# Two pairs of value projections as 1024-wide groups, in a one-core decoder layer

## The chip, the core and the metric

The kernel runs on one core of a Trainium2 chip. A core has a matrix engine (TensorE, called PE in the profile; its weight loads are PEld), a vector engine (DVE), a scalar engine with lookup tables (ACT), a general engine (POOL) and a queue engine (SP). Each works through its own instructions in order and waits for the others by semaphores. PE reads operands from on-chip memory (SBUF) and writes sums to banks of PSUM. The metric is the device time of one execution in microseconds.

## The reference

One layer: a normed input `h` (512 tokens, 1024 features) times one wide matrix `w_in`, whose columns are split for two token mixers; their outputs are gated, merged and projected; then an MLP and a gated extra projection. What matters here:

```python
h = rmsnorm(x, ln1[i])
hq, hk, hv, hr, ha, hatt, hgate = _split_cols(h @ w_in[i], SPLIT_SIZES)
log_a = jax.nn.log_sigmoid((ha @ w_a2[i] + b_a[i]).astype(jnp.float32)) / GLA_TAU
o = gla_mixer(hq..., hk..., hv..., log_a...)     # gated linear attention: 4 heads, values 4 x 256
...
o = o * gla_gn[i] * jax.nn.silu(hr)              # the gate r
...
hatt = hatt.reshape(B, S, N_ATT_GROUPS, 3, ATT_HEADS_PER_GROUP, ATT_HEAD_DIM)   # q, k, v of 3 groups
for g, (win, dil) in enumerate(ATT_GROUPS):      # dilations 1, 4, 16
    o_g, lse_g = dilated_attention(hatt[:, :, g, 0], hatt[:, :, g, 1], hatt[:, :, g, 2], ...)
wts = jax.nn.softmax(jnp.stack(lses, axis=0), axis=0)
o_att = jnp.sum(wts[..., None] * jnp.stack(outs, axis=0), axis=0).reshape(B, S, ATT_W)
```

The columns that the change touches are the values of attention groups 1 and 2 (512 columns each) and the values of the linear attention (1024 columns). The linear attention works in chunks of 64 tokens: per head a running sum of the gate (the "decay"), its exponentials, and queries and keys multiplied by them.

## The kernel before

**Precision.** A float32 product is made of three reduced-precision ones. Each operand is split into `hi` (a rounded copy) and `lo` (what is left), and PE adds hi·hi, lo·hi and hi·lo.

**Weights.** They come as operands of 128 x 1024 (512 KB each). For each, SP issues the load, ACT makes `hi` (L244) and DVE makes `lo` (L239). There are 6 buffers for raw weights, 5 for hi and 4 for lo.

**Groups.** 512 x 1024 x 512 projections are done in seven block products in place of eight (`strassen`, L301). Each of the seven stages has one weight operand: the blocks A11, A12, A22 themselves or sums of blocks (S1 = A21 + A22, S2 = S1 + A11, S3 = A11 + A21, S4 = S2 + A12), against blocks of `h` and their sums (T1 to T4). The order is A11, S1, A22, S2, A12, S4, S3. S1 is a load by SP to which POOL adds a second load in memory (an accumulating DMA, L210); S3 likewise, onto A11 (L221); S2 and S4 are sums on DVE in place (L218, L224). A stage is 24 matmuls of 128 moving columns by 256 (4 inner blocks, 2 halves, 3 products). After stages 0 to 3 ACT copies a bank out (`begin`, L332), after stages 4 to 6 DVE adds the rest (`end`, `add`, L350). Two layouts exist: features on partitions (`quad`), and tokens on partitions (`quadt`, for values), where the weight is the moving operand.

**Order of work.** The program is one stream per engine, laid out by the code itself. `run` (L255) issues matmuls in pieces of eight, and after each piece `step` pops one closure from a list `later` (copies, additions, splits) and, whenever enough columns have been issued (`pace`), takes one step of one of two side generators: scores and softmax, attention values, decay, linear attention. `fetch` issues, whenever an operand is wanted, the lo split of the second operand ahead, the hi split of the third, the sums of the fourth and the loads of the fifth. An engine thus sees splits, evacuations and side work in one fixed order, and a side instruction that waits or takes long holds the splits behind it.

**Around the change.** The groups run in the order k1, q2, k2, v1, v2, v0, gq, gk, gv0, the attention's output projection (`oa`), r0, gv1, r1, then the merge gates. During v1 the scores of groups 1 and 2 are made (`scores12`); at its end their softmax sums go to DRAM and back in another shape (`s_dram`, L713 and L715, both on POOL) and PE transposes them (L719). v1 and v2 are written to DRAM (L658) and read back sorted by residue class (L664). Attention values (`pv`), merge coefficients (`weights`) and `decay` (L851, L852) run beside v0 to gv0, the first linear-attention heads (`gla`, L865) beside `oa` and r0, the last two beside r1. Of a head's steps, the first four prepare: exponentials on ACT (L870, L881, L882), products and copies on DVE (L871 to L895). The gate r is x·sigmoid(x): `silu` issues a sigmoid on ACT (L1051) and two products on DVE (L1055). ACT must load a table whenever it changes between exponential and sigmoid.

## Time and profile before

| what | us |
|---|---|
| median of 3 runs | 965.95 (965.8 to 965.99) |
| the profiled execution | 966.74 |
| its span, first to last instruction | 964.9 |
| PE busy in the span | 956.2 (99%) |
| DVE busy | 745.4 (77%) |
| ACT busy | 537.4 (56%) |
| POOL busy | 104.0 (11%) |
| v1: 144.10 to 171.32 | 27.22 |
| gv0: 270.31 to 293.59 | 23.28 |
| r0: 320.88 to 346.57 | 25.69 |
| gv1: 346.57 to 368.28 | 21.71 |
| r1: 368.28 to 388.53 | 20.25 |

A matmul's line shows its modelled duration; matmuls overlap, so the pace is read from their starts. "Idle before" is what an engine lost ahead of a line's instructions, with what ended most of it. The granted TensorE clock is 0.998 of full speed over the whole execution.

### The profile page before, as it was taken

The numbers are of one execution on the slowest core, as the hardware profiler recorded it, in microseconds if no ns is written. First come the engines' busy times: TensorE is split into PE (matmuls) and PEld (weight loads), VectorE is DVE, ScalarE is ACT, GpSimd is POOL, SyncE is SP. The second block draws the span as 40 slices with busy tenths as digits, with TensorE's granted clock in tenths as the row PEclk, the third lists the DMA queues.
The fourth block names the chain that finished last, engine by engine and source line by source line (L and its number), as shares of the span: only waits on it lengthen the run. The fifth ranks groups of instructions, "written<-read, shape, count | busy, mean of one in ns | idle before, by whom it ended". The sixth has DMA issues, their size and how long they took to land.

```text
span 964.9 us, 16746 instructions
## 1 busy us (share of the span) xinstructions
PE 956.2 (99%) x6732; PEld 893.7 (93%) x6732; DVE 745.4 (77%) x1068; ACT 537.4 (56%) x878; POOL 104.0 (11%) x145
## 2 busy tenths in 40 slices
PE   9999999999999999999999999999999999999997
PEld 7789999999998999999988899999998998988886
DVE  7787879676788769978955788777767899787754
ACT  7346546445666677665732446555655674345633
POOL 0140010420001021013001000010000100000000
PEclk9999999999999999999999999999999999999999
DMA  8565555874446646455536437556654474563102
GB/s 294 159 201 128 153 135 129 236 199 135 110 109 186 164 102 157 113 154 182 169 91 205 119 78 185 153 140 168 170 158 109 113 180 103 132 196 108 44 1 88
DMA packets 41470, 138.93 MB, mean 144 GB/s; under 512 B 5363, under 2 KB 6975, under 8 KB 41392
## 3 DMA queue, kind: packets, MB, share of 16 engines
q1 hardware_dynamic: 27936, 93.29, 29.6%
q0 software_dynamic: 12160, 42.20, 22.1%
q10 hardware_dynamic: 1296, 2.36, 0.7%
q8 instruction: 53, 0.87, 0.4%
q14 instruction: 25, 0.20, 0.1%
HBM read 131.50 MB, written 8.17 MB: 145 GB/s over the span
## 4 chain that ended last, share of the span: by engine, by line
PE 97%; DVE 1%; issue 1%; DMA 1%; ACT 0%; SPq 0%; POOLq 0%; POOL 0%; DVEq 0%; ACTq 0%
PE mmt L258 84%; PE smt L258 4%; PE smt L863 1%; PE smt L803 1%; PE smt L728 1%; DMA u<-in_xT_dram 1%; PE mmt L478 1%; PE mmt L479 0%; PE mmt L477 0%; PE smt L701 0%; PE smt L820 0%; PE smt L819 0%; PE smt L809 0%; PE smt L700 0%; PE smt L991 0%
## 5 line engine op out<-in xcount | busy, mean ns | idle before, releaser
L258 PE MATMUL mmt<-ur,hi 128*128 128x256 f32 (+1 forms) x3152 | 645.3, 302 | 0.0
L258 PEld LDWEIGHTS mmt<-ur,hi 128*128 128x128 f32 x3152 | 506.0, 188 | 24.8 <-issue 1.9
L258 PE MATMUL mmt<-ur,lo 128*128 128x256 f32 (+1 forms) x1576 | 476.9, 303 | 0.0
L239 DVE TENSOR_TENSOR lo<-w,hi 128x1024 fp32r<-128x1024 f32 x251 | 304.2, 1218 | 49.5 <-PE mmt L258 32.1
L244 ACT ACTIVATE hi<-w 128x1024 fp32r<-128x1024 f32 x251 | 262.5, 1054 | 93.2 <-PE mmt L258 28.0
L258 PEld LDWEIGHTS mmt<-ur,lo 128*128 128x128 f32 x1576 | 296.8, 188 | 11.9 <-issue 0.4
L258 PE MATMUL mmt<-hi,ur 128*128 128x256 f32 (+3 forms) x736 | 153.7, 305 | 0.0
L357 ACT ACTIVATE ur<-u 128x512 fp32r<-128x512 f32 x132 | 78.5, 624 | 105.3 <-DVE u L1098 30.9
L258 PEld LDWEIGHTS mmt<-hi,ur 128*128 128x128 f32 x736 | 118.5, 189 | 5.6
L350 DVE TENSOR_TENSOR u<-u,mmt 128x512 f32<-128x512 f32 (+1 forms) x124 | 78.3, 657 | 44.8 <-PE mmt L258 44.6
L258 PE MATMUL mmt<-lo,ur 128*128 128x256 f32 (+3 forms) x368 | 112.2, 305 | 0.0
L365 DVE TENSOR_TENSOR ur<-u,ur 128x512 fp32r<-128x512 f32 x131 | 86.2, 684 | 17.6 <-ACT ur L357 16.9
L332 ACT ACTIVATE u<-mmt 128x512 f32<-128x512 f32 x104 | 61.6, 592 | 55.8 <-PE mmt L258 55.5
L258 PEld LDWEIGHTS mmt<-lo,ur 128*128 128x128 f32 x368 | 69.4, 188 | 2.7
L221 POOL DMA_DIRECT2D w<-in_wts_dram x28 | 24.9, 890 | 356.2 <-DVE w L218 258.3
L210 POOL DMA_DIRECT2D w<-in_wts_dram x28 | 25.8, 921 | 276.5 <-DVE ur L365 52.8
L258 PE MATMUL smt<-ur,hi 128*128 128x512 f32 x144 | 44.7, 390 | 0.1
L224 DVE TENSOR_TENSOR w<-w 128x1024 f32<-128x1024 f32 x28 | 34.3, 1225 | 1.0
L218 DVE TENSOR_TENSOR w<-w 128x1024 f32<-128x1024 f32 x28 | 34.3, 1225 | 1.0
L258 PEld LDWEIGHTS smt<-ur,hi 128*128 128x128 f32 x144 | 26.9, 188 | 6.0 <-DVE ur L365 0.5
L258 PE MATMUL smt<-ur,lo 128*128 128x512 f32 x72 | 28.2, 391 | 0.0
L390 ACT ACTIVATE u<-u 128x512 f32<-128x512 f32 x24 | 14.9, 622 | 16.5 <-DVE u L1179 16.5
(210 smaller groups left out, 715.0 us busy)
## 6 DMA issues: line engine op xcount, KB each, us to landing
w<-in_wts_dram SPq DMA_DIRECT2D x167, 512.0 KB, 4.2
w<-in_wts_dram POOLq DMA_DIRECT2D x56, 512.0 KB, 5.8
u<-in_xT_dram SPq DMA_DIRECT2D x8, 256.0 KB, 5.1
v_dram<-u POOLq DMA_DIRECT2D x8, 256.0 KB, 6.2
u<-v_dram POOLq DMA_DIRECT2D x8, 256.0 KB, 6.6
y_dram<-u ACTq DMA_DIRECT2D x8, 256.0 KB, 2.4
u<-y_dram POOLq DMA_DIRECT2D x8, 256.0 KB, 6.0
u<-in_xT_dram POOLq DMA_DIRECT2D x8, 256.0 KB, 8.6
```

The lines of the kernel that those rows point to most:

```text
L210: GP.dma_start(w, wts[UNIT[f"{q}.A22"]], accum_op=OP.add)
L218: V.tensor_tensor(w, w, raw[f"{q}.A11"], op=OP.add)
L221: GP.dma_start(w, wts[UNIT[f"{q}.A21"]], accum_op=OP.add)
L224: V.tensor_tensor(w, w, raw[f"{q}.A12"], op=OP.add)
L239: V.tensor_tensor(lo, w, hi.bitcast(F32), op=OP.subtract)
L244: S.activation(hi, w, AF.Copy)
L258: TE.matmul(o, lhsT=l, rhs=r, start=a, stop=b, skip_group_check=shared)
L332: S.activation(sums[c], bank[b], AF.Copy, scale=-scale if c[0] else scale)
L350: V.tensor_tensor(out, s, ps, op=OP.subtract if m else OP.add)
L357: S.activation(hi, x, AF.Copy)
L365: V.tensor_tensor(lo, x, hi.bitcast(F32), op=OP.subtract)
L390: S.activation(t, x, AF.Square, scale=1.0 / 32.0)
```

## The change

v1 and v2 become one group `v12`, gv0 and gv1 one group `gv`, each of 1024 features with tokens on partitions. A new function `wide` does the seven products with weight operands of twice the width: two units each (`.0`, `.1`), moving rows of 512 columns, two PSUM banks for each accumulator, and a `step` after every three matmuls. The order of its products is A11, S1, S2, A12, S3, S4, A22. S3 is no longer summed onto the loaded A11, but comes by a load of its own on SP (A11 again) with POOL's accumulation of A21 on it; the table `EARLY` says how many operands ahead the accumulating loads are issued.

The moved work: `gla(0)` and `gla(1)` are put beside gv (before: beside `oa`), `gla(2)` and `gla(3)` beside `oa` and r0 (before: beside r1). They wait in the program for the decay and the values they need. The values of the attention groups are kept in two DRAM buffers. `scores12` has one more `yield` per head. The third sum operand T3 is split into buffers that q1 leaves.

```diff
+    def quadw(name, src, cs):
+        for m, k in ((0, 0), (1, 0), (1, 1), (0, 1)):
+            for i in range(2):
+                u.append((f"{name}.A{m + 1}{k + 1}.{i}", "quadw", src, 2 * i + k, cs[m]))
...
-    quad("v1", "w_in", att_col(1, 2), "quadt")
-    quad("v2", "w_in", att_col(2, 2), "quadt")
+    quadw("v12", "w_in", (att_col(1, 2), att_col(2, 2)))
...
-    quad("gv0", "w_in", GV, "quadt")
+    quadw("gv", "w_in", (GV, GV + 512))
...
-    quad("gv1", "w_in", GV + 512, "quadt")
...
+WIDE = (("A11", "B11", "a"), ("S1", "T1", "c"), ("S2", "T2", "a"), ("A12", "B21", "b"), ("S3", "T3", "a"),
+        ("S4", "B22", "c"), ("A22", "T4", "a"))
+WBEGIN = {0: ((0, 0), "a"), 1: ((1, 1), "c"), 2: ((0, 1), "a")}
+WEND = {3: ((0, 0), "b"), 4: ((1, 1), "a"), 5: ((0, 1), "c"), 6: ((1, 0), "a")}
...
-EARLY = {max(i - LEAD, 0): n[:-4] for n, i in OPERAND.items() if n.endswith(".A11")}
+def early():
+    after_wide = False
+    for n, i in OPERAND.items():
+        q, _, what = n.partition(".")
+        if what == "S1":
+            EARLY.setdefault(max(i - (4 if after_wide else 7), 0), []).append((n, f"{q}.A21", f"{q}.A22"))
+            after_wide = False
+        elif what[:3] == "S1.":
+            EARLY.setdefault(i - 4, []).append((n, f"{q}.A21.{what[3:]}", f"{q}.A22.{what[3:]}"))
+            after_wide = True
+        elif what[:3] == "S3.":
+            EARLY.setdefault(i - 2, []).append((n, f"{q}.A11.{what[3:]}", f"{q}.A21.{what[3:]}"))
...
-            step(PIECE * r.shape[-1])
+            step(n * r.shape[-1])
...
+    def wide(name, xo, finish):
...
+        for i, (op, xname, b) in enumerate(WIDE):
+            fresh = b not in bank
+            if fresh:
+                bank[b] = [smt() if b == "b" else mmt() for _ in range(2)]
+            for pr in range(4):
+                wh, wl = weight(f"{name}.{op}.{pr // 2}")
+                xh, xl = xo(xname, pr)
+                r = slice((pr % 2) * 512, (pr % 2 + 1) * 512)
+                mms = []
+                for n in range(2):
+                    c = slice(n * P, (n + 1) * P)
+                    for k, (l, w) in enumerate(((xh, wh), (xl, wh), (xh, wl))):
+                        mms.append((bank[b][n], l[:, c], w[:, r], fresh and not pr and not k, pr == 3 and k == 2))
+                run(mms, 3, shared=True)
+            if i in WBEGIN:
+                (m, t), b = WBEGIN[i]
+                later[0:0] = [begin(m, t, n, b) for n in range(2)]
+            if i in WEND:
+                (m, t), b = WEND[i]
+                later.extend(end(m, t, n, b) for n in range(2))
...
     def gla(h):
+        while len(gb_) <= h:
+            yield
...
+        while len(gv) < 8:
+            yield
+        if h == 2:
+            for p in range(4):
+                split_later(gv[1, p], gv, (1, p))
...
-    gv = [values("gv0", True)]
-    drain()
+    gv = {}
+    side.extend(gla(h) for h in range(2))
+    values_parts("gv", gv)
+    flush()
     pace[0] = 4096
-    side.extend(gla(h) for h in range(2))
+    side.extend(gla(h) for h in range(2, 4))
...
-    gv.append(values("gv1", True))
-    flush()
-    side.extend(gla(h) for h in range(2, 4))
```

How the order of instructions changes at three places (line numbers of the changed kernel: L239 the accumulating load, before L210; L272 the lo split, before L239; L277 the hi split, before L244).

On POOL, where the softmax sums leave for DRAM (`s_dram`), before:

```order
L210 DMA w_1500<-in_wts_dram 128x1024
L221 DMA w_1437<-in_wts_dram 128x1024
L210 DMA w_1807<-in_wts_dram 128x1024
L713 DMA s_dram_1841<-st12_323 128x8x4
L715 DMA u_1843<-s_dram_1841 32x128
L658 DMA v_dram_1600<-u_1672 128x2x256
L221 DMA w_1714<-in_wts_dram 128x1024
```

and with the change, where w_1805 is the first sum S1 of the group v0, and the two loads ahead of it are the S3 of v12:

```order
L239 DMA w_1640<-in_wts_dram 128x1024
L239 DMA w_1678<-in_wts_dram 128x1024
L239 DMA w_1805<-in_wts_dram 128x1024
L814 DMA s_dram_1824<-st12_326 128x8x4
L816 DMA u_1826<-s_dram_1824 32x128
L759 DMA v0_dram_1596<-u_1686 128x512
```

Before, the load ahead of `s_dram` was one of v2's; now it is one of v0's, into a buffer of v12.

On DVE in gv, with the change: the lo splits of A12.1 (lo_3111), S3.0, S3.1 and S4.0 (lo_3195), the two sums for S4 (L248), and between them the preparation of head 1 (L974 to L998, before L871 to L895):

```order
L272 TENSOR_TENSOR lo_3111<-w_3023,hi_3079 128x1024
L974 TENSOR_TENSOR u_3128<-u_2660 128x4x64
L976 TENSOR_TENSOR u_3129<-u_2660 128x4x64
L272 TENSOR_TENSOR lo_3135<-w_2990,hi_3113 128x1024
L248 TENSOR_TENSOR w_2618<-w_2618,w_2993 128x1024
L981 COPY dec_3150<-u_3127 128x8
L982 TENSOR_TENSOR u_2242<-u_2242,u_3127 128x512
L272 TENSOR_TENSOR lo_3164<-w_3020,hi_3137 128x1024
L248 TENSOR_TENSOR w_2669<-w_2669,w_3023 128x1024
L991 TENSOR_TENSOR u_3175<-u_2611,u_3128 128x512
L992 TENSOR_TENSOR u_2611<-u_2611,u_3129 128x512
```

Before, these rows of heads 0 and 1 stood behind the last lo split of gv0, among oa's.

On ACT at the end of r0, before: one table load ahead of r0's sigmoids (L1051):

```order
L244 ACTIVATE hi_3886<-w_3462 128x1024
L1051 ACT_TABLE_LOAD
L1051 ACTIVATE u_3921<-u_3724 128x512
L964 ACTIVATE u_3862,gsq_3860<-smt_3866 128x256 x2
L244 ACTIVATE hi_3950<-w_3839 128x1024
L1051 ACTIVATE u_3973<-u_3850 128x512
```

and with the change (L1163 is the sigmoid, L973 the first exponential of heads 2 and 3, L984 the next one):

```order
L1163 ACT_TABLE_LOAD
L1163 ACTIVATE u_3863<-u_3686 128x512
L973 ACT_TABLE_LOAD
L973 ACTIVATE u_3875<-u_2736 128x512
L277 ACTIVATE hi_3883<-w_3809 128x1024
L1163 ACT_TABLE_LOAD
L1163 ACTIVATE u_3906<-u_3820 128x512
L973 ACT_TABLE_LOAD
L973 ACTIVATE u_3908<-u_2797 128x512
L1163 ACT_TABLE_LOAD
L1163 ACTIVATE u_3926<-u_3739 128x512
L1163 ACTIVATE u_3928<-u_3777 128x512
```

The exponentials of the two heads now stand between the sigmoids, each behind a table load of its own.

More of the change, by code (lines that the diff above doesn't have):

```diff
@@ L126, in operand_order @@
             names += [f"{name[:-3]}{a}" for a, _, _ in STAGES]
+        elif name.endswith("A11.0"):
+            names += [f"{name[:-5]}{a}.{i}" for a, _, _ in WIDE for i in range(2)]
     return names
@@ L189, in step, with flush @@
                 side.insert(min(WAYS - 1, len(side)), g)
+    def flush():
+        while later:
+            later.pop(0)()
     def drain():
@@ L206, in prepare @@
         name = OPERANDS[i]
-        if i in EARLY:
-            q = EARLY[i]
-            w = raw[f"{q}.S1"] = load(f"{q}.A21")
-            GP.dma_start(w, wts[UNIT[f"{q}.A22"]], accum_op=OP.add)
+        for n, a, b in EARLY.get(i, ()):
+            w = raw[n] = load(a)
+            GP.dma_start(w, wts[UNIT[b]], accum_op=OP.add)
         if name in UNIT:
@@ L214, in sums @@
     def sums(i):
-        q, _, what = OPERANDS[i].rpartition(".")
-        if what == "S2":
+        q, _, what = OPERANDS[i].partition(".")
+        if what[:3] in ("S2.", "S4."):
+            a, b = ("S1", "A11") if what[1] == "2" else ("S2", "A12")
+            w = raw[OPERANDS[i]] = raw[f"{q}.{a}{what[2:]}"]
+            V.tensor_tensor(w, w, raw[f"{q}.{b}{what[2:]}"], op=OP.add)
+        elif what == "S2":
             w = raw[f"{q}.S2"] = raw[f"{q}.S1"]
@@ L534, in xsums @@
         yield from sums(lambda g, p, o: V.tensor_tensor(t3[g][:, o], x(g, p, 1, 1), x(g, p, 0, 1), op=OP.subtract))
-        yield from splits("T3", t3)
+        while not q1_done:
+            yield
+        for g in range(2):
+            for p in range(2):
+                S.activation(xs[4 * g + 2 * p][0][:, halves(1)], t3[g][:, halves(p)], AF.Copy)
+        yield
+        for g in range(2):
+            for p in range(2):
+                hi, lo = cols(xs[4 * g + 2 * p], halves(1))
+                V.tensor_tensor(lo, t3[g][:, halves(p)], hi.bitcast(F32), op=OP.subtract)
+        yield
+    q1_done = []
     def xs_op(name, pr):
+        if name == "T3":
+            return cols(xs[2 * pr], halves(1))
         if name in ("B11", "B21", "B22"):
@@ L898, in gla @@
         yield
-        vh = [cols(gv[h // 2][h % 2, p // 2], halves(p % 2)) for p in range(4)]
+        while len(gv) < 8:
+            yield
+        if h == 2:
+            for p in range(4):
+                split_later(gv[1, p], gv, (1, p))
+        while not all(isinstance(gv[h // 2, p], tuple) for p in range(4)):
+            yield
+        vh = [cols(gv[h // 2, p], halves(h % 2)) for p in range(4)]
         kc = slice(0, 3 * P)
```

64 lines of the change are left out of this document (43 added, 21 removed).

## The prediction

> **What bounds the kernel now.** I read the page's totals first, then its chain of waits, then the costliest groups with what ended their idle time.
>
> ```profile
> span 964.9 us, 16746 instructions
> ...
> PE 956.2 (99%) x6732; PEld 893.7 (93%) x6732; DVE 745.4 (77%) x1068; ACT 537.4 (56%) x878; POOL 104.0 (11%) x145
> ...
> PE 97%; DVE 1%; issue 1%; DMA 1%; ACT 0%; SPq 0%; POOLq 0%; POOL 0%; DVEq 0%; ACTq 0%
> ...
> L258 PE MATMUL mmt<-ur,hi 128*128 128x256 f32 (+1 forms) x3152 | 645.3, 302 | 0.0
> ...
> L239 DVE TENSOR_TENSOR lo<-w,hi 128x1024 fp32r<-128x1024 f32 x251 | 304.2, 1218 | 49.5 <-PE mmt L258 32.1
> L244 ACT ACTIVATE hi<-w 128x1024 fp32r<-128x1024 f32 x251 | 262.5, 1054 | 93.2 <-PE mmt L258 28.0
> ```
>
> PE is busy 99% of the span, the chain is PE for 97% of it, and its main matmul line never waited (0.0 us). So every stall of PE that the change creates is added to the end, and the only gain there can be is PE time. VectorE and ScalarE make the operands, and part of their idle time is spent waiting for PE, so they run ahead. DVE has far less room than the 77% suggests in the stretches that the change rebuilds:
>
> ```profile
> core 0: us, PE busy (x) PEld busy (x) DVE busy (x) ACT busy (x) POOL busy (x), PEclk, DMA share, GB/s
> 144.10:171.32 27.22, 27.22 (x235) 27.22 (x233) 25.27 (x32) 17.01 (x43) 3.73 (x6) 1.00 0.52 119
> 270.31:293.59 23.28, 23.28 (x201) 23.28 (x199) 19.75 (x24) 12.28 (x18) 0.00 (x0) 1.00 0.59 152
> 320.88:346.57 25.69, 25.69 (x218) 25.69 (x217) 16.88 (x26) 14.97 (x29) 1.72 (x2) 1.00 0.53 131
> 368.28:388.53 20.25, 20.25 (x173) 20.25 (x172) 19.82 (x36) 16.59 (x26) 1.87 (x3) 1.00 0.59 153
> ```
>
> These are v1, gv0, r0 and r1 (stretch, length, busy time and instructions of each engine). Granted clock is 1.00 in all four.
>
> **The gain: 336 pairs of matmuls become single ones.** 672 matmuls of 128x256 become 336 of 128x512. Matmuls are pipelined, so I take the distance between starts, not the duration of one.
>
> ```profile
> 211.70 0.40 PE L258 MATMUL mmt<-ur,hi 128*128 128x256 f32 x2
> ...
> 213.12 0.28 PE L258 MATMUL mmt<-ur,hi 128*128 128x256 f32 x1
> ...
> 299.74 0.61 PE L258 MATMUL mmt<-ur,hi 128*128 128x512 f32 x2
> ...
> 301.10 0.39 PE L258 MATMUL mmt<-ur,hi 128*128 128x512 f32 x1
> ```
>
> From 211.70 to 213.12 start 12 narrow ones, 118.3 ns each; the whole of v0 (168 in about 20.0 us) makes 119.0; I take 118.7. From 299.74 to 301.10 start six wide ones: 226.7 ns. A pair costs 237.4, so a wide one saves 10.7 ns, and 336 save **3.6 us** (3.2 to 3.8 by 118.3 and 119.0). The 10.7 is a small difference of two large numbers, but both are read in the same way. The Trainium skill, "TensorE: Matmul & The Clock Gate", section "Back-to-back issue gap", gives N/2.4 + 2.5 ns, by which a pair would save 2.5 ns and the change 0.8 us. The rows disagree (118.7 where that gives 109.2), and the measurement decides. By that rule the forecast below would end 2.8 us later.
>
> Evacuations fall too: from 8 on DVE and 8 on ACT to 6 and 8 per group of the same work, each about 0.6 us, on engines beside PE: worth nothing by itself. The four more 512 KB loads run on SP's queue, where the DMA share is 0.5 to 0.6 in these stretches: nothing for bandwidth. But they, and the moved preparation, reorder three in-order queues, and there I find PE late.
>
> **Stall 1, POOL in v12.** POOL's accumulating load for v0's first sum now stands ahead of the small round trip through DRAM that brings the softmax sums to PE.
>
> ```profile
> w<-in_wts_dram SPq DMA_DIRECT2D x167, 512.0 KB, 4.2
> ...
> u<-s_dram POOLq DMA_DIRECT2D x1, 16.0 KB, 3.1
> ...
> 151.80 0.87 POOL L210 DMA_DIRECT2D w<-in_wts_dram  x1 [8.24 <-DVE lo L239]
> 165.36 0.96 POOL L713 DMA_DIRECT2D s_dram<-st  x1 [12.69 <-DVE lo L239]
> 169.42 0.54 POOL L715 DMA_DIRECT2D u<-s_dram  x1 [3.10 <-PE mmt L258]
> ...
> 174.29 0.24 PE L719 MATMUL smt<-ident,u 32*128 32x32 f32 x1
> ```
>
> Before, the read went out 4.06 us after the write, landed 3.1 later (172.5), and PE's transpose came at 174.29: 1.8 us of cover. In v12 the accumulate waits for SP's load into the buffer that S3.0 leaves, so for DVE's lo split of S3.0. v12 starts at 144.10 as v1 did; v1's 27.22 us less 168 x 0.1187 leave 7.28 for the score matmuls. That split needs the lo buffer of S2.0, which PE leaves after matmul 60: 144.10 + 7.28 + 60 x 0.2267 = 165.0. With one split (1.2) it ends at 166.2; with the last scores' additions and A12's split also ahead of it, at 169.2; I take 167.9, since those stand ahead in DVE's order. Plus 4.2 (load), 0.87 (issue), 4.06 and 3.1: the sums land at 180.1. PE asks after matmul 120: 144.10 + 7.28 + 27.2 = 178.6. Stall **1.5 us**, from 0 (166.2) to 2.8 (169.2). The merge coefficients behind it come as much later; their cover in gq takes that, to within a few tenths that I leave in the range.
>
> **Stall 2, DVE in gv.** The four decay sums and the preparation of heads 0 and 1 of the linear attention now stand between gv's lo splits; before, gv0 held the decay alone and the preparation ran in oa.
>
> ```profile
> 276.77 1.11 DVE L822 TENSOR_TENSOR u<-smt,u 128x512 f32<-128x512 f32 x1 [2.46 <-PE smt L820]
> 277.79 1.22 DVE L239 TENSOR_TENSOR lo<-w,hi 128x1024 fp32r<-128x1024 f32 x1
> 278.93 0.68 DVE L851 TENSOR_TENSOR u<-u 128x512 f32<-128x512 f32 x1
> ...
> 281.37 0.69 DVE L851 TENSOR_TENSOR u<-u 128x512 f32<-128x512 f32 x1
> ...
> 283.23 0.67 DVE L851 TENSOR_TENSOR u<-u 128x512 f32<-128x512 f32 x1
> ...
> 299.14 0.42 DVE L871 TENSOR_TENSOR u<-u 128x256 f32<-128x256 f32 x1
> ...
> 300.48 0.16 DVE L878 COPY dec<-u 128x8 f32<-128x8 f32 x1
> ...
> 301.84 1.21 DVE L239 TENSOR_TENSOR lo<-w,hi 128x1024 fp32r<-128x1024 f32 x1
> ...
> 305.24 0.67 DVE L888 TENSOR_TENSOR u<-u 128x512 f32<-128x512 f32 x1
> ...
> 307.16 0.28 DVE L893 COPY u<-u 128x256 f32<-128x256 f32 x1
> ...
> 307.77 0.28 DVE L893 COPY u<-u 128x256 f32<-128x256 f32 x1
> ```
>
> By distance of starts: a lo split or a 128x1024 sum 1.14 us; one decay 1.86 (281.37 to 283.23); of one head the two L871/L873 0.67 (half of 299.14 to 300.48), the dec copy and its product 0.68, L888 to L891 1.92 (305.24 to 307.16; I count 2.0, the mean with the other head), L893 to L895 0.61. From the addition of the last attention values on (276.77, 6.46 after the section's start; 0.13 earlier with twelve wide matmuls in place of 24 narrow ones: 6.3) DVE's order holds: that addition, a wait of 0.7 for ACT's hi and a lo, together 2.4; then up to A12.1's lo four splits (4.6), four decays (7.4), head 0's whole preparation (0.67 + 0.68 + 2.0 + 0.61 = 4.0): 16.0. A12.1's lo ends 24.7 after the start. PE asks for it at its matmul 86: 86 x 0.2267 + 3.34 (what 23.28 leaves beside 168 narrow ones) = 22.8. Late by 1.9. From there to S4.0's lo: two splits, two S4 sums, head 1's preparation (4.0) and the split itself: 9.7, ends 34.4; PE asks at 122 x 0.2267 + 3.34 = 31.0. Late by 3.4 in all, the first 1.9 included. After it DVE has few rows and recovers. I take **3.3 us**. Every wait inside would add; a start earlier by one row would take 1: 2.3 to 4.2.
>
> **Stall 3, ACT and DVE where r0 meets r1.** The preparation of heads 2 and 3 moves into r0's end. Its exponentials alternate with r0's sigmoids: the order has six table loads within 14 ACT rows, where before one stood ahead of all four sigmoids of r0.
>
> ```profile
> 267.21 0.60 ACT L795 ACTIVATE u<-smt 128x512 f32<-128x512 f32 x1 [0.26 <-PE smt L803]
> 267.83 1.28 ACT L848 ACT_TABLE_LOAD   x1
> 269.12 0.63 ACT L848 ACTIVATE u<-u 128x512 f32<-128x512 f32 x1
> ...
> 341.57 0.68 DVE L350 TENSOR_TENSOR u<-u,mmt 128x512 f32<-128x512 f32 x1
> ...
> 342.34 0.63 ACT L1051 ACTIVATE u<-u 128x512 f32<-128x512 f32 x1 [2.20 <-DVE u L350]
> 342.88 0.37 ACT L964 ACTIVATE u<-smt 128x256 f32<-128x256 f32 x1
> ...
> 376.88 0.41 ACT L881 ACTIVATE u<-u 128x256 f32<-128x256 f32 x1
> ...
> 378.11 1.04 ACT L244 ACTIVATE hi<-w 128x1024 fp32r<-128x1024 f32 x1
> ```
>
> A load takes 1.28, with 0.01 to 0.02 around it; a sigmoid or a whole exponential 0.54; four of the narrow exponentials 1.23; a hi split 0.95. Take t = 0 at r0's sixth stage (a stage is 24 x 0.1187 = 2.85; before at 320.88 + 25.69 - 5.70 = 340.87). The first sigmoid starts at t = 1.5 (342.34), and then: sigmoid 0.54, load, exponential, hi, load, sigmoid, load, exponential, load, two sigmoids: 10.8. DVE's gate products wait for these (0.7) and r1's A22 lo stands behind them: ends at 12.7, where PE asks at 11.4 + 0.24 = 11.6: late 1.1. ACT goes on: hi, load, eight narrow exponentials (2.5), hi, and only then the copy (0.6) that empties r1's first bank: 17.0. PE adds into that bank from its fourth stage, 14.2 + 1.1 = 15.3: late by 1.7 more. DVE, now with the preparation between its splits, is 0.3 late for S4. Together 3.1; closures are issued once in eight matmuls (0.95), which can push the chain as far: 1.5 to 4.2, I take **3.2**. The Trainium skill, "ScalarE: Activation LUTs", section "What ACT_TABLE_LOAD costs", adds about 1.38 us of draining to each switch. The rows of this case show none of it (267.83 + 1.28 against 269.12).
>
> Where I find no stall: k1, where the third operand's splits wait for q1's end, v0, oa, and from gb0 on; DVE is freed by the 21.7 us of gv1 that no longer stand between r0 and r1 and goes back to waiting for PE within two stages.
>
> **Sum.** -3.6 + 1.5 + 3.3 + 3.2 = +4.4 us. The span of 964.9 becomes 969.3. The profiled execution took 966.74, 0.8 over the median of 965.95, against which the forecast is 965.95 + 4.4 = **970.4 us**. With all three stalls at their low or high ends (3.8, 11.2): 966.2 to 973.6.
>
> **Rivals.**
> (a) The whole gain, no stall: the splits, the loads and the sigmoids lead by more than I count. For it: 32.1 us of DVE's waits before lo splits and 28.0 of ACT's before hi splits are for PE, so both do run ahead. Against it: DVE was busy for 19.75 of gv0's 23.28, and ACT's chain at r0 has no slack in it to lead with, since it starts at a sum that PE finishes. 965.95 - 3.6 = 962.4, or up to 964.0 with 1.6 of stalls.
> (b) Only part of it stalls: gv alone (965.7), r0 with r1 alone (965.6), or two of them at the low end (-3.6 + 2.3 + 1.5 = 966.2). It needs that DVE in gv or ACT at r0 lead by a whole operand. 964 to 967.9: no change that can be told.
> (c) Table loads hold ACT longer where they alternate than where one stands alone; the one place is r0's end, and it decides as soon as each costs double, six more times 1.28 on the chain: 970.4 + 7.7 = 978. No row speaks for it. The draining that the Trainium skill states in "ScalarE: Activation LUTs", "What ACT_TABLE_LOAD costs", would come to 970.4 + 6 x 1.38 = 978.7.
> (d) The change doesn't give the saving that it is made of: the wide matmuls now alternate between two banks in runs of three, and if that lengthens their pitch to the pair's 237, the sum is 974.0. The rows at 299.74, of runs of three in one bank, speak against it as far as they go.
>
> **How the numbers follow.** Forecast 0.54, (a) 0.18, (b) 0.18, (c) 0.04, (d) 0.06. What can be told from no change is 0.2%, 1.9 us: 964.0 to 967.9. Faster is (a) and a little of (b): 0.21. Same is the rest of (b) and the lowest of the forecast: 0.19. Slower: 0.60. The range 963.2 to 974.2 takes in the forecast's own 966.2 to 973.6, (b), (d) and the upper part of (a).
>
> **What would show it.** PE's starts in v12 and gv 226 to 228 ns apart. PE idle before a transpose near 178 us put down to the DRAM read; in gv two idle times of PE put down to L239's successor, at A12 and S4; at r0's end six table loads within 15 us, PE idle at r1's third stage (lo) and fourth (ACT's copy of the bank). It is wrong if PE is still at 99% with no idle time above 0.5 us in these places (then a), or if one of the three shows none (b), and wrong in kind if PE waits somewhere else, such as for the four new loads.

## The result: slower by 1.5%

The changed kernel takes 980.2 us in the median (979.76 to 981.18), the kernel before 965.88; the ratio is 1.015 (95% interval 1.0133 to 1.0168). The forecast was 970.4, at most 974.2. The direction was right; the loss of 14.3 us is more than three times the 4.4 forecast. The profiled execution took 980.02, its span 978.2.

From the page of the changed kernel (totals, chain, one of the groups):

```profile
span 978.2 us, 16084 instructions
...
PE 959.0 (98%) x6396; PEld 879.7 (90%) x6396; DVE 743.4 (76%) x1066; ACT 543.2 (56%) x884; POOL 98.7 (10%) x145
...
PE 93%; DVE 3%; ACT 2%; issue 2%; DMA 0%; POOLq 0%; POOL 0%; DVEq 0%; SPq 0%; ACTq 0%
...
L291 PE MATMUL mmt<-ur,lo 128*128 128x256 f32 (+1 forms) x1576 | 478.0, 303 | 2.3 <-DVE lo L272 2.2
```

PE's share of the chain fell from 97% to 93%, and a matmul line that had never waited now waits for lo splits. PE issues 336 matmuls fewer and yet is busy 2.8 us longer: some of them ran slowly. The table of PE's waits (line, what it waited for, us in total, times, longest) shows where it stood still:

```profile
PE smt L820 <- issue: 6.2, 1, 6.2
PE mmt L291 <- DVE lo L272: 3.1, 2, 2.2
PE smt L291 <- DVE lo L272: 1.4, 1, 1.4
```

L820 is the transpose of the softmax sums in v12. Two of the three lo waits lie in gv (1.4 and 0.9), one in r1 (2.2). Those are the three places that the prediction named. By stretches, cut at the first matmul of each group:

| stretch | before | after | difference |
|---|---|---|---|
| v1 and v2, now v12 | 47.56 | 55.08 | +7.5 |
| v0, gq, gk | 78.64 | 79.41 | +0.8 |
| gv0, oa, r0, gv1, r1, now gv, oa, r0, r1 | 118.22 | 122.78 | +4.6 |
| gb0 to ga1 | 92.26 | 94.55 | +2.3 |

That is 15.1 us. The last row is not a loss of its own: 19 small products that ran in gv1 and r1 before (16 transposes of the outputs of heads 0 and 1, and 3 of head 2's preparation) now run there, and make these 2.3 us. The work ahead of v12 and behind ga1 is the same; the start of a span, up to v12, varies by some two microseconds between executions with the same instructions (142.78 to 144.93 us in the traces shown here), so the differences of spans (13.3) and of medians (14.3) need not be 15.1.

**In v12** the wait is followed by something that the prediction had not priced. PE's rows around it, and the windows of the same stretch (stretch, length, PE's busy time and instructions, granted clock, DMA share, GB/s):

```profile
177.58 0.40 PE L291 MATMUL mmt<-lo,ur 128*128 128x512 f32 x1
184.16 0.28 PE L820 MATMUL smt<-ident,u 32*128 32x32 f32 x1 [6.18 <-issue]
184.37 1.22 PE L291 MATMUL mmt<-hi,ur 128*128 128x512 f32 x2
...
185.82 1.05 PE L291 MATMUL mmt<-hi,ur 128*128 128x512 f32 x2
```

```profile
177.60:184.00 6.40, 0.38 (x2) 0.88 0.71 229
184.00:188.00 4.00, 3.84 (x10) 0.50 0.85 177
188.00:197.86 9.86, 9.86 (x42) 0.94 0.60 192
```

After 6.2 us without work PE's clock is at half: from 184.37 to 189.23, for about 5 us, matmuls that were 232 ns apart are 427 apart. That costs 2.3 us (ten intervals at 195 ns more and one at 362 more). The Trainium skill states this in "TensorE: Matmul & The Clock Gate", section "HAM oscillation — how this bites in real kernels": no idle gaps of PE over about 3.4 us, or the clock drops to half. This gap agrees.

POOL's rows show why PE waited; under them are the landing times of the round trip (issue to landing):

```profile
170.93 0.86 POOL L239 DMA_DIRECT2D w<-in_wts_dram  x1 [18.42 <-DMA w<-in_wts_dram]
171.47 1.28 POOL L814 DMA_DIRECT2D s_dram<-st  x1
182.15 0.55 POOL L816 DMA_DIRECT2D u<-s_dram  x1 [9.40 <-DMA s_dram<-st]
```

```profile
s_dram<-st POOLq DMA_DIRECT2D x1, 16.0 KB, 10.1
u<-s_dram POOLq DMA_DIRECT2D x1, 16.0 KB, 1.9
```

POOL did issue the accumulating load first, at about the time forecast (170.9; forecast 172.1). But the 16 KB write behind it took 10.1 us to land, where it took 3.5 before. The read then went out at 182.15 and landed 1.9 later; PE's transpose came at 184.16.

**In gv** DVE's rows at PE's first wait are those that the prediction summed:

```profile
300.25 0.27 DVE L996 COPY u<-u 128x256 f32<-128x256 f32 x1
...
300.85 1.22 DVE L272 TENSOR_TENSOR lo<-w,hi 128x1024 fp32r<-128x1024 f32 x1
```

```profile
302.12 0.50 PE L291 MATMUL smt<-lo,ur 128*128 128x512 f32 x1 [1.37 <-DVE lo L272]
...
311.69 0.50 PE L291 MATMUL mmt<-lo,ur 128*128 128x512 f32 x1 [0.93 <-DVE lo L272]
```

gv starts at 277.26. A12.1's lo ends at 302.07, 24.8 after it (forecast 24.7).

**At r0 and r1** there are six table loads in 14 us, and each sigmoid but one starts when the load ahead of it ends (that one waits 0.29 us more, for its sum):

```profile
370.45 1.28 ACT L1163 ACT_TABLE_LOAD   x1
371.74 0.63 ACT L1163 ACTIVATE u<-u 128x512 f32<-128x512 f32 x1
372.39 1.28 ACT L973 ACT_TABLE_LOAD   x1
...
375.29 1.28 ACT L1163 ACT_TABLE_LOAD   x1
376.86 0.63 ACT L1163 ACTIVATE u<-u 128x512 f32<-128x512 f32 x1 [0.29 <-DVE u L418]
...
379.46 1.28 ACT L1163 ACT_TABLE_LOAD   x1
380.75 1.15 ACT L1163 ACTIVATE u<-u 128x512 f32<-128x512 f32 x2
...
382.87 1.28 ACT L984 ACT_TABLE_LOAD   x1
```

```profile
381.42 1.43 DVE L1167 TENSOR_TENSOR u<-u 128x256 f32<-128x256 f32 x4 [1.94 <-ACT u L1163]
382.77 1.22 DVE L272 TENSOR_TENSOR lo<-w,hi 128x1024 fp32r<-128x1024 f32 x1
```

```profile
384.04 0.58 PE L291 MATMUL mmt<-ur,lo 128*128 128x256 f32 x1 [2.22 <-DVE lo L272]
```

The last row is PE at r1's third stage: it waits for the lo split, which stands behind gate products that wait for the last sigmoids. Behind this wait, too, the clock was at half (stretch, length, PE's busy time and instructions, clock, DMA share, GB/s):

```profile
380.43:383.84 3.41, 1.39 (x12) 1.00 0.31 61
383.84:387.25 3.41, 3.21 (x15) 0.50 0.52 154
```

### The profile page after: what moved, and what is told of

The parts are those of the page before. It is cut to its first block, busy times and chain, and to the rows that moved or that the text cites. A ratio compares the mean times of both kernels' runs of the same rounds, so it can differ in the third digit from the quotient of the medians.

```text
span 978.2 us, 16084 instructions
## 1 busy us (share of the span) xinstructions
PE 959.0 (98%) x6396; PEld 879.7 (90%) x6396; DVE 743.4 (76%) x1066; ACT 543.2 (56%) x884; POOL 98.7 (10%) x145
## 4 chain that ended last, share of the span: by engine, by line
PE 93%; DVE 3%; ACT 2%; issue 2%; DMA 0%; POOLq 0%; POOL 0%; DVEq 0%; SPq 0%; ACTq 0%
PE mmt L291 79%; PE smt L291 5%; PE smt L964 1%; DVE lo L272 1%; PE smt L904 1%; PE smt L829 1%; PE mmt L546 1%; PE mmt L547 1%; PE mmt L545 1%; PE smt L921 0%; PE smt L801 0%; PE smt L920 0%; PE smt L800 0%; PE smt L910 0%; PE smt L1502 0%
## 5 line engine op out<-in xcount | busy, mean ns | idle before, releaser
L291 PEld LDWEIGHTS mmt<-ur,hi 128*128 128x128 f32 x3152 | 506.9, 189 | 24.8 <-issue 1.9
L272 DVE TENSOR_TENSOR lo<-w,hi 128x1024 fp32r<-128x1024 f32 x251 | 304.5, 1219 | 60.7 <-PE mmt L291 36.6
L277 ACT ACTIVATE hi<-w 128x1024 fp32r<-128x1024 f32 x251 | 262.3, 1054 | 113.2 <-PE mmt L291 39.8
L291 PE MATMUL mmt<-hi,ur 128*128 128x512 f32 (+3 forms) x480 | 135.1, 367 | 0.0
L418 DVE TENSOR_TENSOR u<-u,mmt 128x512 f32<-128x512 f32 (+1 forms) x116 | 73.1, 655 | 38.7 <-PE mmt L291 38.5
L291 PEld LDWEIGHTS mmt<-hi,ur 128*128 128x128 f32 x480 | 86.2, 191 | 14.0 <-issue 0.4
L291 PE MATMUL mmt<-lo,ur 128*128 128x512 f32 (+3 forms) x240 | 87.4, 364 | 0.9 <-DVE lo L272 0.9
L365 ACT ACTIVATE u<-mmt 128x512 f32<-128x512 f32 x88 | 52.1, 592 | 50.4 <-PE mmt L291 49.0
L239 POOL DMA_DIRECT2D w<-in_wts_dram x32 | 29.4, 960 | 316.8 <-DMA w<-in_wts_dram 171.3
L291 PEld LDWEIGHTS mmt<-lo,ur 128*128 128x128 f32 x240 | 45.7, 191 | 8.5 <-DVE lo L272 1.4
L257 DVE TENSOR_TENSOR w<-w 128x1024 f32<-128x1024 f32 x24 | 29.4, 1225 | 0.8
L251 DVE TENSOR_TENSOR w<-w 128x1024 f32<-128x1024 f32 x24 | 29.4, 1225 | 0.8
```

The costliest lines, as they stand in the source:

```text
L239: GP.dma_start(w, wts[UNIT[b]], accum_op=OP.add)
L251: V.tensor_tensor(w, w, raw[f"{q}.A11"], op=OP.add)
L257: V.tensor_tensor(w, w, raw[f"{q}.A12"], op=OP.add)
L272: V.tensor_tensor(lo, w, hi.bitcast(F32), op=OP.subtract)
L277: S.activation(hi, w, AF.Copy)
L291: TE.matmul(o, lhsT=l, rhs=r, start=a, stop=b, skip_group_check=shared)
```

## The experiments

All are set against runs of the kernel before on the same chip (medians 965.88 to 966.1). The variants ran on different chips, and what stands ahead of v12 varies by up to 2 us, so a difference of that size between two variants is read from the stretches, from v12's first matmul on.

### The round trip: which queue, or which order

In the code, `GP` issues on POOL's queue and `S` on ACT's.

```diff
-        GP.dma_start(s_dram..., st12...)
+        S.dma_start(s_dram..., st12...)
```

> The changed kernel, but the write of the softmax sums to DRAM is issued on ACT's queue in place of POOL's; POOL's accumulating load and the read back stay where they are. Theory A (the small write lies behind the 512 KB accumulate in POOL's own DMA queue): it lands about 3 us after its issue as before, PE's wait of 6.2 us before the transpose goes, and with it the half clock of the 4 us behind it (2 us): 980.2 - 8 = 972. Theory B (the write is slow because all DMA engines are full of weight loads by SP): it still takes some 10 us, and the time stays at 979 to 981.

Measured: 977.72 us, ratio 1.0121 (1.0106 to 1.0136). Neither theory's number. The write went out earlier (168.8) on ACT's queue, ahead of the accumulate in time, and landed in 6.0 us, though the DMA engines were then 0.97 busy; then the read, on POOL's queue behind the accumulate, took 7.9:

```profile
s_dram<-st ACTq DMA_DIRECT2D x1, 16.0 KB, 6.0
u<-s_dram POOLq DMA_DIRECT2D x1, 16.0 KB, 7.9
```

The window from the write's issue to its landing (stretch, length, POOL's busy time, clock, DMA share, GB/s):

```profile
168.80:174.80 6.00, 0.58 (x1) 1.00 0.97 208
```

So the place behind the accumulate moved from the write to the read and with it the long landing. PE waited 3.5 us, 2.7 less, and the clock was at half for 3.4 us behind it: v12 took 51.67 us, 3.4 less than with the change. The median gained only 2.5; the profiled execution began v12 at 144.73, 2.0 later than that of the change, which hides as much in its span.

```diff
-            EARLY.setdefault(max(i - (4 if after_wide else 7), 0), ...
+            EARLY.setdefault(max(i - (3 if after_wide else 7), 0), ...
```

> The changed kernel with the first sum of the group after a wide one issued 3 operands ahead in place of 4, which puts its accumulating load behind the round trip of the softmax sums on POOL; the write stays on POOL's queue. Theory A: no load lies ahead of the write, it lands in 3 to 4 us, PE's 6.2 us and the half clock go: 972, less if v0's first sum comes late (then PE waits at v0's second stage). Theory B: the write is as slow as before: 979 to 981.

Measured: 972.45 us, ratio 1.0066 (1.0051 to 1.0081), 7.75 less than the change, as theory A has it. Write and read now have nothing ahead of them on POOL's queue:

```profile
s_dram<-st POOLq DMA_DIRECT2D x1, 16.0 KB, 5.8
u<-s_dram POOLq DMA_DIRECT2D x1, 16.0 KB, 4.7
```

PE waits 0.2 us at the transpose, the clock stays up, and v12 takes 46.82 us in place of 55.08. What theory B holds is there too, only smaller. The same windows, from the write's issue to its landing, of the kernel before, of this one and of the change:

```profile
165.36:168.90 3.54, 0.96 (x1) 1.00 0.45 132
```

```profile
167.35:173.20 5.85, 0.96 (x1) 1.00 0.85 207
```

```profile
171.47:181.60 10.13, 1.27 (x2) 1.00 1.00 307
```

Before, the DMA engines were busy for 0.45 of that time; in the wide group for 0.85 even with nothing ahead on POOL's queue, and then the write takes 5.8 in place of 3.5. The remaining step to 10.1 is the place behind the accumulate: on ACT's queue, in the run before this one, the write took 6.0 with the engines 0.97 busy, nearly as full as the 1.00 of the change. The Trainium skill says in "DMA: Bandwidth & Descriptors", section "Two DMAs through the same engine are not ordered", that the descriptors of one queue of one DMA engine start in order; the rows agree, with 10.1 behind a 512 KB load and 5.8 without one.

### What the idle clock costs

24 useless matmuls of 128x512 in front of the transpose, into the bank that it overwrites:

```diff
         pst = smt()
+        for _ in range(24):
+            TE.matmul(pst, lhsT=xs[0][0][:, 0:P], rhs=xs[0][0], start=True, stop=True)
         TE.transpose(pst[:, 0:32], s_row...
```

> The changed kernel with 24 useless 128x512 matmuls (5.4 us) put in front of PE's wait before the transpose in v12, into the bank that the transpose then overwrites. The wait of 6.2 us shrinks to under 1 us without ending sooner. If the idle PE loses its clock and pays for it afterwards, the clock stays at 1.0 in the 4 us behind and the time falls by about 2 us: 978.2. If the clock behind the wait has another cause, no change: 980.2.

Measured: 977.78 to 980.1 us in three executions, too far apart to tell the theories from each other. The one trace has a granted clock of 0.556 from end to end (1585 us), and PE did not wait at the transpose in it, so it says nothing of the cover. A second form has the 24 as one sum over eight tiles:

```diff
+        for i in range(24):
+            TE.matmul(pst, lhsT=xs[i % 8][0][:, 0:P], rhs=xs[i % 8][0], start=i == 0, stop=i == 23)
```

> The changed kernel with 24 useless 128x512 matmuls (5.4 us) in front of PE's wait in v12, as in the run before that did so, but as one sum over eight stationary tiles. If the idle clock costs 2 us behind the wait: 978.2 and a clock of 1.0 in the 4 us behind it; if not: 980.2.

Measured: 978.98 us, ratio 1.0126 (1.0111 to 1.0142). The two windows that answer to those above:

```profile
178.00:184.00 6.00, 6.00 (x27) 1.00 0.99 294
184.00:188.00 4.00, 3.48 (x16) 1.00 0.49 158
```

The clock stays at 1.00 and v12 takes 52.62 us, 2.5 less than without the cover: in the stretch the clock theory holds to a few tenths. The median gained only 1.2. In the profiled execution, the work from v12's first matmul to the gated output's projection took 348.7 us in place of 351.8, but v12 began at 144.86, 2.1 later than in that of the change; the other executions have no trace.

### The table loads at r1

```diff
-        S.activation(g, s, AF.Sigmoid)
+        S.activation(g, s, AF.Exp)
```

> The changed kernel with exp in place of the sigmoid in the gate r, so that the computed gate is another function (left out: the sigmoid), but no table has to be changed between the exponentials of heads 2 and 3 and the gate; order and lengths are otherwise the same. If the six table loads make the wait at the start of r1, ACT's chain is 5 us shorter, the 2.4 us wait and the 1.7 us of half clock behind it go: 980.2 - 4 = 976. If it is DVE's moved preparation, the wait stays at 1 us or more: 978.5 or above.

Measured: 977.23 us, ratio 1.0114 (1.0097 to 1.0131), 3.0 less. r1 takes 21.73 us in place of 24.31, where the bare 168 matmuls take 19.94. So the loads make 2.6 of the 4.4 us lost at r1; the other 1.8 lie around two waits (0.7 and 0.5 us by PE's rows) for lo splits behind the heads' preparation. Each theory had a part.

The same without leaving anything out, together with the accumulating load behind the round trip:

```diff
-        S.activation(g, s, AF.Sigmoid)
+        S.activation(g, s, AF.Tanh)          # s is now x/2, by the evacuation's scale
...
-                V.tensor_tensor(outs[n], s[:, halves(n)], g[:, halves(n)], op=OP.mult)
+                V.scalar_tensor_tensor(out=outs[n], in0=g[:, halves(n)], scalar=1.0, in1=s[:, halves(n)], op0=OP.add, op1=OP.mult)
```

> The changed kernel with the accumulating load behind the round trip, and the gate r computed as x/2 (1 + tanh(x/2)) in place of x sigmoid(x): the same function, but tanh and exp need no table change. If the loads and not the order make r1's wait, it falls by the 2.7 us that the exp gate showed in r1: 972.4 - 2.7 = 969.7. If the longer form of the additions on DVE takes it back: 971 to 972.5.

Measured: 969.75 us, ratio 1.0039 (1.0026 to 1.0053), as forecast for the loads. The longer form on DVE costs nothing visible: r1 takes 21.71 us, as with the exp gate.

### All heads back in their places

```diff
-    side.extend(gla(h) for h in range(2))
     values_parts("gv", gv)
-    flush()
+    drain()
     pace[0] = 4096
-    side.extend(gla(h) for h in range(2, 4))
+    side.extend(gla(h) for h in range(2))
...
     side.extend(gla_out(h) for h in range(2))
+    side.extend(gla(h) for h in range(2, 4))
     gates("r", 1, rg, silu)
```

> The changed kernel with the linear attention's heads back where they were: 0 and 1 beside the attention's projection, 2 and 3 beside r1; the wide groups stay. If the moved preparation is what delays DVE's splits in gv (1.5 + 1.1 us) and ACT at r0's end (2.4 us and 1.7 us at half clock), both go and the wait before the transpose in v12 stays: 980.2 - 6.5 = 973.7. If the wide group's own splits and sums are too dense for DVE in gv, that wait stays: 976 or above.

Measured: 982.72 us, ratio 1.0173 (1.0158 to 1.0188): slower than the change itself, against every expectation (by 1.6 us from v12's first matmul to the end, in the profiled executions). The waits in gv and at r1 did go (gv 42.38 us, r1 21.67). They came back later:

```profile
PE mmt L291 <- ACT ur L425: 2.4, 1, 2.4
PE mmt L291 <- DVE lo L272: 1.5, 1, 1.5
...
PE mmt L291 <- DVE ur L433: 0.8, 1, 0.8
```

The first and the last are at the gated output's projection, which now starts before the heads' outputs are split, and it runs its first matmuls at half clock (47.62 us in place of 43.54). The middle one is in ga0. Before the change, gv1 stood between r0 and r1, 21.7 us in which PE needed no result of the heads. With gv1 gone from there, heads 2 and 3 either start early, in DVE's and ACT's fullest stretches, or end late.

### The pitch of a wide matmul

```diff
+        o = 0 if OPERANDS[i][:4] == "v12." else SHIFT if ...   # SHIFT is 32 elements
...
+                    for k, (l, w) in enumerate(((xh, wh), (xh, wl), (xl, wh)) if name == "gv" else ((xh, wh), (xl, wh), (xh, wl))):
```

> The changed kernel; in v12 the split weights start at offset 0 of their buffers in place of 32 elements, in gv the three products come as hi.hi, hi.lo, lo.hi, so that a stationary tile stands for two matmuls in a row. Read are the distances of starts in the two groups, 232.4 ns in both with the change (227 in groups whose moving operand is the token side). If the place of the weights in their buffers makes the 5.6 ns, v12 falls to 227 and gv stays; if it is the reload of the stationary tile, gv falls to 227 and v12 stays; if it is that the moving operand is the freshly split weights, both stay at 232.

One execution, for its trace: in v12 148 intervals have a mean of 227.1 ns, in gv 159 have 232.5. From PE's rows of this run, two triples in v12 and two in gv:

```profile
167.31 0.39 PE L291 MATMUL smt<-lo,ur 128*128 128x512 f32 x1
...
168.67 0.39 PE L291 MATMUL smt<-lo,ur 128*128 128x512 f32 x1
```

```profile
290.70 0.40 PE L291 MATMUL mmt<-lo,ur 128*128 128x512 f32 x1
...
292.08 0.40 PE L291 MATMUL mmt<-lo,ur 128*128 128x512 f32 x1
```

Six intervals take 1.36 us in v12 and 1.38 in gv; the means over the groups resolve what two rows hardly do. The offset of 32 elements, which the narrow groups' weights have in their buffers, is what costs a wide matmul 5.3 ns; the order of the three products does nothing (gv has 232.6 with the change, 232.5 here). Why that offset costs so much is not known from these runs. The first theory holds.

### One part alone

The attention values as a wide group, the accumulating load behind the round trip; the linear attention's values and heads as before the change.

> Half of the change: the attention values as one wide group (with the accumulating load behind the round trip, as in the run before that did so), the linear attention's values as gv0 and gv1 and its heads where they were. If each part's loss is its own, v12 gains 168 x (237.4 - 232.4) ns = 0.8 us and gq loses up to 1.1 us behind the later merge coefficients: 965.5 to 966.5, no change. If the wide group also delays what follows through the moved queue, 967 or above; if the whole gain of a wide group shows, 964.2.

Measured: 966.26 us, ratio 1.0001 (0.9992 to 1.001). v12 takes 47.06 us (v1 and v2: 47.56), gq 32.68 (31.32). With the weights at offset 0:

> The attention values alone as a wide group (966.26 without the next edit), with its weights at offset 0: 168 x 5.3 ns = 0.9 us less, 965.4, if the pitch is all that changes; 966.3 if the time saved in v12 is only waited for in gq, where the merge coefficients are late (32.7 in place of 31.3 us).

Measured: 965.99 us, ratio 1.0 (0.9991 to 1.0009). v12 takes 46.23, but gq 33.11: the second expectation, the time saved is waited for in gq. What gq waits for are the merge coefficients, whose own round trip through DRAM stands behind the reads of the second group's values on POOL. With those reads put behind it:

```diff
-                    GP.dma_start(v, v_dram[m]...)     # at once
+                    late.append(reads)                # second group: after the coefficients' read is issued
```

> The attention values alone as a wide group with offset 0 (965.99), with the four reads of the second group's values issued on POOL behind the merge coefficients' round trip in place of ahead of it. If gq is late (33.1 us in place of 31.3) because the coefficients stand behind reads that wait for writes to land, gq falls to 31.4 and the time to 964.3; if the coefficients are late from the softmax sums on, gq stays above 32.5 and the time at 965.5 to 966.

Measured: 965.5 us, ratio 0.9993 (0.9984 to 1.0002): no difference that can be told. The write now goes out at 196.7 in place of 208.2, but takes until 209.1 to be read on:

```profile
196.74 0.89 POOL L877 DMA_DIRECT2D k_dram<-u  x1
209.06 0.80 POOL L878 DMA_DIRECT2D cc<-k_dram  x1 [11.43 <-DMA k_dram<-u]
```

gq still takes 32.40 us, and the 0.7 us that it gained v0 lost (20.76 in place of 20.09), most of it in a wait of 0.4 for ACT's copy of a bank. Half of the theory holds (the reads were ahead), but the 8 KB write now took 12.0 us to land, behind the first group's four 256 KB reads, an accumulating load and two 256 KB writes; that it pays their time, as in v12, is argued from the order alone. Whether the coefficients alone make gq's 1.1 us was not tested further.

### The whole change, mended

Both wide groups, tanh gate, round trip first, offset 0, and the side work in gv at half the pace:

```diff
+    pace[0] = 4096
     values_parts("gv", gv)
```

> The kernel with tanh and the accumulating load behind the round trip (969.75), with two more edits. The wide groups' weights at offset 0: 336 x 5.3 ns = 1.8 us less (227 ns in both groups). And side work in gv at one step per 4096 columns in place of 2048. If what delays the splits in gv is the density of the heads' preparation, PE's two waits there (1.5 and 1.1 us) go, as DVE has room behind S4: 969.75 - 1.8 - 2.6 = 965.3. If the room isn't there, the waits move to S4 and A22 and it stays at 968; if the heads come too late for the output gate, PE waits there, as it did for og with all heads put back, and it is 969 or above.

Measured: 970.22 us, ratio 1.004 (1.0027 to 1.0053). The pitch fell to 227 in both groups and r1 was bare (19.94), but gv took 45.80: the two waits became one, for an addition that frees a bank, and the next splits of heads 2 and 3 made PE wait 1.7 us in gb0.

```profile
308.38 0.70 PE L291 MATMUL mmt<-hi,ur 128*128 128x512 f32 x2 [2.41 <-DVE u L418]
```

Behind this wait the clock was at half again. The nine executions lie between 967.61 and 973.16 us, the three longest with a mean clock of 0.994, the two shortest with 0.997 and 0.998, so part of the spread is how long the clock was down.

> The same with side work in r1 at one step per 6144 columns in place of 4096. In r1 PE still waited 0.9 and 0.8 us for lo splits behind the preparation of heads 2 and 3. If density is the cause there too: 965.3 - 1.7 = 963.6. If the later heads cost as much behind (gb0, gb1): 965.3.

Measured (with pace 6144 in r1): 974.19 us, ratio 1.0078 (1.0065 to 1.0092). Both rivals and more: in the profiled execution, the shortest of the four (972.19), PE waited in gb0 (1.4 us) and at the first matmul of the gated output's projection (2.1 us, for the heads' outputs). Slowing the preparation only moves it.

Then the decay was taken out of gv, in place of the slower pace; the reads of the second group's values stand behind the coefficients' round trip, as in the run above:

```diff
-    side.extend([pv(0), pv(1), pv(2), decay(), pv(3)])
+    side.extend([pv(0), decay(), pv(1), pv(2), pv(3)])
```

> The whole change with all that the runs point to: accumulating load behind the softmax round trip, tanh gate, offset 0, deferred reads, and the decay made in gq and gk (its generator put ahead of the second head's attention values), so that gv holds the heads' preparation without the four decays (7.4 us of DVE). If gv's waits come from the sum of decay and preparation: gv without waits, 969.75 - 1.8 (pitch) - 1.1 (gq) - 2.7 (gv) = 964.2, with r1's 1.7 us of waits left. If the preparation alone is too dense, the waits move within gv as they did at the slower pace: 967 or above. If gq and gk have no room for the decay on DVE (they are busy 22 of 32 and 21 of 27 us): waits there, 966 or above.

Measured: 966.17 us, ratio 1.0003 (0.9994 to 1.0011). In gv PE waits no more; the longest waits left between v12 and ga1 are two for splits, both in r1:

```profile
PE mmt L291 <- DVE lo L272: 1.5, 2, 1.0
```

So gv's waits came from decay and preparation together, as the first theory has it: with the preparation taken out (all heads back) they went too. The forecast of 964.2 was missed by 2, though the profiled execution's span is 963.7 against 964.9 before: from v12's first matmul to ga1's last the work takes 336.9 us, before 336.7, so that what the pitch gives (3.5) goes into r1's 2.1 and 1.6 of losses that weren't followed one by one.

```diff
         V.tensor_tensor(k, k, ea, op=OP.mult)
+        if h > 1:
+            yield
```

> The kernel with all edits (966.2), with one more break in the preparation of heads 2 and 3, between the products of queries and keys and the scaling of the pair sums, so that less of it stands between two lo splits of r1. PE waited 1.15 and 0.66 us for these splits; by the DVE rows they come 0.6 and 1.3 us earlier: 966.2 - 1.2 = 965.0. If what is put off only makes a later split or the heads' output late: 966 or above.

Measured: 967.99 us, ratio 1.0025 (1.0012 to 1.0038). r1 fell by 1.1 us (22.04 to 20.97), as forecast, but gb0 took 1.9 more for one split that is now behind:

```profile
395.67 0.39 PE L291 MATMUL mmt<-ur,lo 128*128 128x256 f32 x1 [1.80 <-DVE lo L272]
```

No version beat the kernel before by what can be told (0.2%).

## Why the prediction was right and where it failed

- **What bounds the kernel**: right. PE's stalls went straight to the end, and none came from a place that was not named, apart from tenths in gq that were left to the range.
- **The gain, "336 save 3.6 us"**: mis-sized. Its pitch came from wide matmuls of another kind, with the token side moving. In the changed kernel the moving operand is the weight tile at an offset of 32 elements, 232.4 ns in place of 226.7, so a pair saves 5.0 ns and the change 1.7 us. The rival (d) named a longer pitch, but by the change of banks; the run on the pitch shows the offset. At offset 0 the saving is 10.3 ns per pair, close to the forecast 10.7. (By its pitch of 118.3 the low end of the gain is 3.3, not 3.2.)
- **Stall 1, 1.5 us**: the step that failed. The place was right (the accumulating load ahead of the round trip), the price of the round trip was not. Its step "Plus 4.2 (load), 0.87 (issue), 4.06 and 3.1" took the round trip at the price it had with nothing under way ahead of it in its queue and the DMA engines 0.45 busy, after "nothing for bandwidth" had dismissed the loads. Behind the 512 KB accumulate the write took 10.1, so PE waited 6.2; and the half clock behind the wait, 2.3, was no term at all. Together, by v12's length and the 0.8 us that its pitch saves, 8.4 where 1.5 stood. With the accumulate behind the round trip 7.75 came back. This is the step that put the time out of the range: with 1.5 in place of the 8.4 the kernel would have ended at about 973.
- **Stall 2, 3.3 us**: right, place and size. A12.1's lo was forecast at 24.7 after gv's start and came at 24.8, S4.0's at 34.4 as forecast; PE waited at both, 2.6 us by the intervals (1.5 and 1.1) or 2.3 by the waits. It is less than 3.3 since the slower matmuls ask later (122 of them, 5.7 ns each, make 0.7 us at S4).
- **Stall 3, 3.2 us**: right in place and cause, low by 1.2. r1 took 24.31 against a bare 19.94. The lo split ended 14.0 after the sixth stage's start (forecast 12.7): for the most part since a table load begins only once the activation ahead of it has ended (0.65 from start to start in place of the 0.54 used, for a hi split 1.06 in place of 0.95), at four places ahead of the last sigmoids, and since one sigmoid waited 0.29 for its sum. The second wait, for ACT's copy of the bank, doesn't show in the changed kernel's trace, because PE ran that stretch at half clock; in the run with the 24 matmuls as one sum, with the clock at 1.0 there, it is in the table of waits, 1.3 us, and r1 is as long (24.39). So either the slow clock or the wait is paid, not both.
- **"Where I find no stall"**: right for k1, v0, oa and from gb0 on. "The cover in gq takes that, to within a few tenths" was low: gq lost 0.75.
- **The rivals**: (a), the splits lead by more than counted, is refuted in gv and at r1 by the rows above, and (b) with it, as all three places showed their waits. (c), loads that cost double where they alternate, is refuted: 1.28 each, with 0.02 around it. The draining of 1.38 us that the Trainium skill states in "ScalarE: Activation LUTs", section "What ACT_TABLE_LOAD costs", is in no row here.
- **The sum**: -1.7 + 8.4 + 2.6 + 4.4 + 0.8 is 14.5, against a median that moved by 14.3 and stretches that grew by 15.1; the last 0.6 is assigned to nothing.

## What to carry to other kernels

A small transfer that PE waits for costs what lies ahead of it in its queue, not its own landing time from another place in the program: before a load is moved on a queue, look for the round trips behind it. And when two groups of work are merged, ask what the time between them had covered: here the 21.7 us of one group between two others had hidden a preparation that afterwards, in none of the versions tried, found a place on DVE where it delayed no split. A pitch is taken from a matmul with the same moving operand at the same place in its buffer.

## What the runs showed of the hardware

- A 128x512 matmul whose moving operand starts 32 elements into its buffer has 232.5 ns from start to start, at the buffer's start 227.1, both in one execution; by stage, the means are 232.1 to 232.7 and 226.6 to 229.2.
- A 16 KB write to DRAM took 3.5, 5.8, 6.0 and 10.1 us to land: with the DMA engines 0.45 busy, 0.85 busy, 0.97 busy but on ACT's queue, and behind a 512 KB accumulating load on the same queue with the engines full.
- PE's clock fell to half after waits of 6.2 and 3.5 us, and matmuls were then 427 ns apart. After a wait of 2.2 us at r1 it fell in some executions and stayed at 1.00 in others, with the same kernel text there; after the waits of 1.4 and 0.9 us it never fell. The 3.4 us that the Trainium skill gives for this ("TensorE: Matmul & The Clock Gate", "What's actually happening") is thus no lower bound on the wait here.
- What decides, by these traces, is how the wait lies to a fixed step of 3.41 us. In every trace but that of 0.556, the clock between the start and the end of the work changes only whole such steps after it first stands at full, and half clock lasts 3.41 or 6.83 us. With the change it is full from 4.96 us on and falls at 182.45 and 383.84, 52 and 111 steps later. At full clock, each step in which PE idled 2.0 us or more was followed by a step at half, and none in which it idled 1.6 or less. The 2.2 us of r1 fell with 2.0 into one step in the change (the rows at 380.43 above); in the run with the 24 matmuls as one sum they are divided, with 1.1 on each side of a boundary, and the clock stays up:

```profile
378.41:381.82 3.41, 2.35 (x20) 1.00 0.57 111
381.82:385.24 3.42, 2.27 (x19) 1.00 0.34 80
```

- tanh and exp run without a table load between them, as the Trainium skill's "ScalarE: Activation LUTs" states in "Table sets: the hidden batching unit": with the tanh gate the r1 stretch fell by 2.6 us, as with exp itself, and in that run a tanh starts at 368.74 and an exponential at 369.28 with no load between.
